# Mixture of softmaxes on one core: joint weights per unit, manual waits, larger edge loads, and the prior in the load queue

## Chip, cores, metric

One core of one Trainium2 chip. The metric is the device time of one execution in microseconds (us), read as the median of several; most executions of one kernel agree within 0.1 to 0.4 us here.

## The reference

```python
# logits [32, 128, 4, 4096] f32, prior [32, 128, 4] f32
prior_probs = softmax(prior, axis=-1)                  # over the 4 heads
softmax     = softmax(logits, axis=-1)                 # over the 4096 words
mixture     = np.sum(prior_probs[..., None] * softmax, axis=2)   # [32, 128, 4096]
```

268 MB are read and 67 MB written, each byte once.

## The kernel before

The 4096 rows are cut into 32 units of 128 rows, one row a partition. A unit is 4 heads x 4096 words = 8 MB of logits; its output is 2 MB. Two load buffers (`ltile`) alternate. ACT takes exp of a head and its sum (`dsum`), DVE the reciprocal, POOL multiplies it with the prior's weight (`coeff`), and DVE adds the weighted head to the output.

```python
def pieces(b):
    return 1 if b == 0 or b >= B - 3 else H        # heads per load: 2 MB pieces at the edges, else 8 MB
def load(b, eng=nc.sync):
    lt = lpool.tile([P, H, V], FP32, name="ltile")
    n = pieces(b)
    for h in range(0, H, n):
        eng.dma_start(out=lt[:, h : h + n], in_=lg[b // J, b % J, :, h : h + n, :])
...
load(0, eng=nc.sync)
nc.scalar.dma_start(out=pr, in_=pv)                # the prior, 64 KB, on ACT's queue
load(1, eng=nc.sync)
... # softmax of the prior on DVE and ACT, transposed to pp
ebuf = cpool.tile([P, 2, V], FP32, name="ebuf")
for b in range(B):
    ...
    if 0 < b < B - 3:
        store(b - 1, eng=nc.scalar)
    for h in range(H):
        et = lt[:, h] if inplace else ebuf[:, h % 2]
        ex = nc.scalar.activation(et, lt[:, h], AF.Exp, accum_out=dsum[:, col])
        ...
        nc.vector.reciprocal(rden[:, col], dsum[:, col])
        if h == 0:
            nc.vector.tensor_scalar(out=acc, in0=et, scalar1=rden[:, col], scalar2=pp[...],
                                    op0=ALU.mult, op1=ALU.mult)
            continue
        nc.gpsimd.tensor_mul(coeff[:, col], rden[:, col], pp[...])
        ... # scalar_tensor_tensor: acc = et * coeff + acc; the very last one in two halves, each stored
    if b + 2 < B:
        load(b + 2)
    if b == B - 3:
        store(b - 1); store(b)                     # from here on SP's queue
    elif b == B - 2:
        store(b)
```

The softmax here doesn't subtract the row's maximum and nothing guards it: scores larger than these inputs give would overflow.

## Time and profile before

| | before |
|---|---|
| time, median | 782.5 us (782.68 in the rounds with the changed kernel) |
| profiled span | 780.6 us |
| DVE, ACT, POOL busy | 68%, 60%, 2% |
| the two data queues, share of 16 DMA engines | 82.2% + 17.6% |
| DMA rate in the middle | 434 GB/s |
| first packet, last packet | 1.0 us, 779.2 us |

How to read it: a packet is one row's piece of a transfer, moved by one of the 16 DMA engines.

### The profile page before, as it was taken

The page shows a single profiled execution, that of the slowest core. Times are in us where ns is not written, and L with a number is a line of the kernel's source. Part 1 is how long each engine was busy: PE and PEld are TensorE (multiplying, and loading weights), DVE is VectorE, ACT ScalarE, POOL GpSimd, SP SyncE. Part 2 cuts the span into 40 slices and gives each one's busy share as a digit, 9 for nine tenths or more (in the row PEclk, how much of TensorE's full clock was granted, in tenths as well). Part 3 has the DMA queues.
Part 4 walks back from the last instruction along what each step waited for, and adds up shares of the span by engine and source line. Part 5 has one row for each costly group of instructions (what it writes and reads, how often), then busy time and mean ns, then how long its engine had stood idle before and what let it go on. Part 6 is the DMA issues. An engine that isn't in the chain of part 4 may idle for free.

```text
span 780.6 us, 853 instructions
## 1 busy us (share of the span) xinstructions
DVE 531.4 (68%) x266; ACT 470.2 (60%) x258; POOL 19.3 (2%) x101
## 2 busy tenths in 40 slices
DVE  5756668656686666866667765677666776668994
ACT  4376555755557655576555775457655567558971
POOL 0000000000000000000000000000000000000000
DMA  9999999999999999999999999999999999999998
GB/s 388 434 454 433 403 470 403 467 407 442 431 415 458 413 460 403 453 421 460 413 442 444 400 459 413 453 424 449 411 456 417 453 416 424 449 413 430 429 429 359
DMA packets 11127, 335.67 MB, mean 430 GB/s; under 512 B 1248, under 2 KB 1248, under 8 KB 1264
## 3 DMA queue, kind: packets, MB, share of 16 engines
q1 hardware_dynamic: 7056, 276.83, 82.2%
q10 hardware_dynamic: 4064, 58.79, 17.6%
q14 instruction: 7, 0.06, 0.0%
HBM read 268.50 MB, written 67.11 MB: 430 GB/s over the span
## 4 chain that ended last, share of the span: by engine, by line
DMA 66%; ACT 14%; DVE 10%; issue 7%; POOL 0%; SPq 0%; DVEq 0%; POOLq 0%; ACTq 0%
DMA ltile<-in_logits_dram 66%; ACT ebuf L135 14%; DVE acc L156 9%; DVE ltile L156 1%; POOL coeff L151 0%; SPq L75 0%; DVE rden L144 0%; DVEq L194 0%; DVE ltile L146 0%; POOLq L194 0%; ACTq L135 0%
## 5 line engine op out<-in xcount | busy, mean ns | idle before, releaser
L135 ACT ACTIVATE ebuf<-ltile 128x4096 f32<-128x4096 f32 x120 | 433.0, 3609 | 281.3 <-DMA ltile<-in_logits_dram 234.5
L156 DVE SCALAR_TENSOR_TENSOR acc<-ebuf,coeff,acc 128x4096 f32<-128x4096 f32 x90 | 403.6, 4484 | 27.3 <-POOL coeff L151 27.3
L144 DVE RECIPROCAL rden<-dsum 128x1 f32<-128x1 f32 x128 | 20.4, 160 | 200.7 <-ACT ebuf L135 200.7
L146 DVE TENSOR_SCALAR acc<-ebuf,rden,pp 128x4096 f32<-128x4096 f32 x30 | 72.4, 2412 | 1.1
L151 POOL TENSOR_TENSOR coeff<-rden,pp 128x1 f32<-128x1 f32 x96 | 18.2, 189 | 746.2 <-DVE rden L144 746.2
L135 ACT ACTIVATE ltile<-ltile 128x4096 f32<-128x4096 f32 x8 | 28.9, 3609 | 4.2 <-DMA ltile<-in_logits_dram 4.2
L156 DVE SCALAR_TENSOR_TENSOR ltile<-ltile,coeff 128x4096 f32<-128x4096 f32 (+1 forms) x7 | 27.0, 3874 | 1.8 <-POOL coeff L151 1.8
L135 ACT ACTIVATION_READ_ACCUMULATOR ebuf<-ltile 128x1 f32 x120 | 22.4, 186 | 0.0
L93 DVE TENSOR_REDUCE pmax<-pr 16x256 f32<-16x1024 f32 x1 | 1.2, 1207 | 7.0 <-DMA pr<-in_prior_dram 7.0
L95 ACT ACTIVATE pr<-pr 16x1024 f32<-16x1024 f32 x1 | 1.1, 1056 | 7.0 <-DVE pr L94 7.0
L146 DVE TENSOR_SCALAR ltile<-ltile,rden,pp 128x4096 f32<-128x4096 f32 x2 | 4.8, 2414 | 0.1
L98 DVE TENSOR_TENSOR pn<-pr,pmax 16x1024 f32<-16x1024 f32 x1 | 1.9, 1945 | 0.1
L95 ACT ACT_TABLE_LOAD x1 | 1.3, 1283 | 1.2 <-PEq L183 1.2
L96 DVE TENSOR_REDUCE pmax<-pr 16x256 f32<-16x1024 f32 x1 | 1.2, 1207 | 1.1 <-ACT pr L95 1.1
L105 DVE STREAM_TRANSPOSE pp<-pn 32x256 f32<-32x256 f32 x4 | 1.7, 435 | 0.1
L97 DVE RECIPROCAL pmax<-pmax 16x256 f32<-16x256 f32 x1 | 1.7, 1741 | 0.0
L135 ACT ACTIVATION_READ_ACCUMULATOR ltile<-ltile 128x1 f32 x8 | 1.5, 186 | 0.0
L94 DVE TENSOR_TENSOR pr<-pr,pmax 16x1024 f32<-16x1024 f32 x1 | 1.2, 1214 | 0.0
L91 POOL MEMSET pn<- 32x1024 f32 x1 | 0.9, 941 | 0.3 <-POOLq L183 0.3
L183 POOL MEMSET const-float32-0.0<- 128x1 f32 x1 | 0.1, 103 | 0.2 <-issue 0.2
L183 POOL MEMSET const-bfloat16-1.0<- 128x1 bf16 x1 | 0.1, 106 | 0.0
L183 POOL MEMSET const-uint8-127<- 128x1 uint8 x1 | 0.1, 106 | 0.0
(1 smaller groups left out, 0.1 us busy)
## 6 DMA issues: line engine op xcount, KB each, us to landing
out_dram<-acc ACTq DMA_DIRECT2D x28, 2048.0 KB, 29.3
ltile<-in_logits_dram SPq DMA_DIRECT2D x16, 2048.0 KB, 20.3
out_dram<-acc SPq DMA_DIRECT2D x2, 2048.0 KB, 32.9
out_dram<-ltile SPq DMA_DIRECT2D x1, 2048.0 KB, 21.2
out_dram<-ltile SPq DMA_DIRECT2D x2, 1024.0 KB, 8.7
ltile<-in_logits_dram SPq DMA_DIRECT2D x28, 32.3
pr<-in_prior_dram ACTq DMA_DIRECT2D x1, 64.0 KB, 6.2
```

The costliest lines, as they stand in the source:

```text
L93: nc.vector.reduce_max(pmax, pr, axis=AX.X)
L94: nc.vector.tensor_sub(pr, pr, pmax.unsqueeze(2).to_broadcast([G, R, H]))
L95: nc.scalar.activation(pr, pr, AF.Exp)
L96: nc.vector.reduce_sum(pmax, pr, axis=AX.X)
L97: nc.vector.reciprocal(pmax, pmax)
L98: nc.vector.tensor_mul(pn[0:G].rearrange("g h r -> g r h"), pr, pmax.unsqueeze(2).to_broadcast([G, R, H]))
L105: nc.vector.transpose(pp[32 * t : 32 * (t + 1)], pq[:, :, :, 32 * t : 32 * (t + 1)])
L135: ex = nc.scalar.activation(et, lt[:, h], AF.Exp, accum_out=dsum[:, col])
L144: nc.vector.reciprocal(rden[:, col], dsum[:, col])
L146: nc.vector.tensor_scalar(out=acc, in0=et, scalar1=rden[:, col], scalar2=pp[:, b % J, h, b // J : b // J + 1], op0=ALU.mult, op1=ALU.mult,)
L151: nc.gpsimd.tensor_mul(coeff[:, col], rden[:, col], pp[:, b % J, h, b // J : b // J + 1])
L156: nc.vector.scalar_tensor_tensor(out=acc[:, cs], in0=et[:, cs], scalar=coeff[:, col], in1=acc[:, cs], op0=ALU.mult, op1=ALU.add,)
```

## The change

Its intent: one reciprocal and one coefficient per unit (per two heads in the last four units), waits declared by hand so that each instruction waits for one or two things only, the first head's exp in place and the other three in three buffers of their own (one in PSUM), pieces of two heads for the edge units, and the prior's load on SP's queue between the two halves of unit 0. The first weighted add of a unit now also frees its load buffer.

```diff
+    nc.at_finalize(early_first_load)
-        return 1 if b == 0 or b >= B - 3 else H
+        if u == 0 or u >= U - 3:
+            cuts = (0, 2, 3, 4) if u == U - 1 else (0, 2, 4)
+        else:
+            cuts = (0, H)
+            if u >= 2:
+                only(ld, adds[u - 2, 0] if h == 0 else exps[u - 2, to - 1])
+            if u == 0 and h == 0:
+                nc.sync.dma_start(out=pr, in_=pv)
-    nc.scalar.dma_start(out=pr, in_=pv)
-    ebuf = cpool.tile([P, 2, V], FP32, name="ebuf")
+    ebuf1 = cpool.tile([P, V], FP32, name="ebuf1")
+    ebuf2 = psum.tile([P, V], FP32, name="ebuf2")
+    ebuf3 = cpool.tile([P, V], FP32, name="ebuf3")
+    obuf = cpool.tile([P, 2, V], FP32, name="obuf")
...
+            def weigh(h, n, *keep):
+                rc = nc.vector.reciprocal(rden[:, u, h : h + n], dsum[:, u, h : h + n])
+                only(rc, exps[u, h + n - 1])
+                mul = nc.gpsimd.tensor_mul(
+                    coeff[:, u, h : h + n], rden[:, u, h : h + n], ppu[:, h : h + n])
+                return only(mul, rc, *keep)
...
+            free = (stores[u - 2],) if bufd and u >= 2 else ()
+            m = H if u < U - 4 else 2
+            for h in range(H):
+                if h == H - 1 and 0 < u < U - 3:
+                    store(u - 1, obuf[:, (u - 1) % 2], nc.scalar)
+                exp(h, *((stores[u - 4],) if late else ()))
+                if (h + 1) % m:
+                    continue
+                g = h + 1 - m
+                mul = weigh(g, m, *(free if g == 0 else ()))
+                ... # the weighted adds of heads g to h
```

`only(ins, *keep)` keeps the waits named and drops the others.

More of the change, by code (lines that the diff above doesn't have):

```diff
@@ L53 @@
     G = B * S // R
-    B = G * J
-    assert G * R == B * S and G <= 32
+    U = G * J
+    assert G * R == B * S and G <= 32 and H == 4
     lg = logits.rearrange("b s h v -> (b s) h v").rearrange("(g p j) h v -> g j p h v", p=P, j=J)
@@ L59 @@
     pv = prior.rearrange("b s h -> (b s) h").rearrange("(g r) h -> g r h", r=R)
-    lpool = ctx.enter_context(tc.tile_pool(name="lpool", bufs=2))
-    apool = ctx.enter_context(tc.tile_pool(name="apool", bufs=2))
     cpool = ctx.enter_context(tc.tile_pool(name="cpool", bufs=1))
-    def pieces(b):
-        return 1 if b == 0 or b >= B - 3 else H
-    ltiles = {}
-    def load(b, eng=nc.sync):
-        lt = lpool.tile([P, H, V], FP32, name="ltile")
-        n = pieces(b)
-        for h in range(0, H, n):
-            eng.dma_start(out=lt[:, h : h + n], in_=lg[b // J, b % J, :, h : h + n, :])
-        ltiles[b] = lt
@@ L78, with only @@
-    accs = {}
-    def store(b, lo=0, hi=V, eng=nc.sync):
-        eng.dma_start(out=ov[b // J, b % J, :, lo:hi], in_=accs[b][:, lo:hi])
-    load(0, eng=nc.sync)
-    nc.at_finalize(early_first_load)
+    psum = ctx.enter_context(tc.tile_pool(name="psum", bufs=1, space=bass.MemoryType.PSUM))
+    before = {}
+    def only(ins, *keep):
+        for k in keep:
+            tc.add_manual_dep(
+                ins.ins,
+                k.ins.name,
+                mybir.DependencyInfo(mybir.DependencyClass.Sync, mybir.DependencyReason.DATA),
+                reason="all that this instruction waits for",
+            )
+        tc.declare_no_dep(
+            ins.ins,
+            group="loop",
+            keep=[k.ins for k in keep] + before.get(ins.ins.engine, []),
+            reason="covered by the waits that are kept",
+        )
+        tc.add_to_no_dep_group("loop", ins.ins)
+        before[ins.ins.engine] = [ins.ins]
+        return ins
@@ new lines, with load @@
+    ltile = cpool.tile([P, 2, H, V], FP32, name="ltile")
+    loads = {}
+    exps = {}
+    adds = {}
+    stores = {}
+    def load(u):
+        if u == 0 or u >= U - 3:
+            cuts = (0, 2, 3, 4) if u == U - 1 else (0, 2, 4)
+        else:
+            cuts = (0, H)
+        for h, to in zip(cuts, cuts[1:]):
+            ld = nc.sync.dma_start(
+                out=ltile[:, u % 2, h:to], in_=lg[u // J, u % J, :, h:to, :]
+            )
+            if u >= 2:
+                only(ld, adds[u - 2, 0] if h == 0 else exps[u - 2, to - 1])
+            else:
+                only(ld)
+            for k in range(h, to):
+                loads[u, k] = ld
+            if u == 0 and h == 0:
+                nc.sync.dma_start(out=pr, in_=pv)
@@ L87, with store @@
+    def store(u, acc, eng, lo=0, hi=V):
+        st = eng.dma_start(out=ov[u // J, u % J, :, lo:hi], in_=acc[:, lo:hi])
+        stores[u] = only(st, adds[u, H - 1])
     pr = cpool.tile([G, R, H], FP32, name="pr")
-    nc.scalar.dma_start(out=pr, in_=pv)
-    load(1, eng=nc.sync)
     pn = cpool.tile([32, H, R], FP32, name="pn")
-    nc.gpsimd.memset(pn, 0.0)
     pmax = cpool.tile([G, R], FP32, name="pmax")
-    nc.vector.reduce_max(pmax, pr, axis=AX.X)
-    nc.vector.tensor_sub(pr, pr, pmax.unsqueeze(2).to_broadcast([G, R, H]))
@@ L95 @@
-    nc.scalar.activation(pr, pr, AF.Exp)
-    nc.vector.reduce_sum(pmax, pr, axis=AX.X)
-    nc.vector.reciprocal(pmax, pmax)
-    nc.vector.tensor_mul(
-        pn[0:G].rearrange("g h r -> g r h"), pr, pmax.unsqueeze(2).to_broadcast([G, R, H])
-    )
-    pq = pn.rearrange("g h (p j) -> g j h p", j=J)
-    pp = cpool.tile([P, J, H, 32], FP32, name="pp")
-    for t in range(P // 32):
-        nc.vector.transpose(pp[32 * t : 32 * (t + 1)], pq[:, :, :, 32 * t : 32 * (t + 1)])
-    NCHUNK = 2
-    dsum = cpool.tile([P, B * H], FP32, name="dsum")
@@ L111 @@
-    rden = cpool.tile([P, B * H], FP32, name="rden")
-    coeff = cpool.tile([P, B * H], FP32, name="coeff")
-    ebuf = cpool.tile([P, 2, V], FP32, name="ebuf")
-    exps = []
-    for b in range(B):
-        last = b == B - 1
-        inplace = b >= B - 2
-        lt = ltiles.pop(b)
-        if not inplace:
-            accs[b] = apool.tile([P, V], FP32, name="acc")
-        else:
-            accs[b] = lt[:, 0]
-        acc = accs[b]
-        if 0 < b < B - 3:
-            store(b - 1, eng=nc.scalar)
-        for h in range(H):
-            split = last and h == H - 1
-            i = b * H + h
-            col = slice(i, i + 1)
-            et = lt[:, h] if inplace else ebuf[:, h % 2]
-            ex = nc.scalar.activation(et, lt[:, h], AF.Exp, accum_out=dsum[:, col])
-            if h == 0:
-                tc.keep_in_program_order(ex)
-            if not inplace:
-                if len(exps) >= 2:
-                    tc.declare_no_dep(ex.ins, exps[-2], reason="covered by the sum")
-                exps.append(ex.ins)
-            nc.vector.reciprocal(rden[:, col], dsum[:, col])
-            if h == 0:
-                nc.vector.tensor_scalar(
-                    out=acc, in0=et, scalar1=rden[:, col], scalar2=pp[:, b % J, h, b // J : b // J + 1],
-                    op0=ALU.mult, op1=ALU.mult,
-                )
-                continue
-            nc.gpsimd.tensor_mul(coeff[:, col], rden[:, col], pp[:, b % J, h, b // J : b // J + 1])
-            n = NCHUNK if split else 1
-            w = V // n
-            for c in range(n):
-                cs = slice(c * w, (c + 1) * w)
-                nc.vector.scalar_tensor_tensor(
-                    out=acc[:, cs], in0=et[:, cs], scalar=coeff[:, col], in1=acc[:, cs],
-                    op0=ALU.mult, op1=ALU.add,
-                )
-                if split:
-                    store(b, c * w, (c + 1) * w)
-        if b + 2 < B:
-            load(b + 2)
-        if b == B - 3:
-            store(b - 1)
-            store(b)
-        elif b == B - 2:
-            store(b)
@@ new lines, with exp, add @@
+    pp = cpool.tile([P, J, H, 32], FP32, name="pp")
+    dsum = cpool.tile([P, U, H], FP32, name="dsum")
+    rden = cpool.tile([P, U, H], FP32, name="rden")
+    coeff = cpool.tile([P, U, H], FP32, name="coeff")
+    ebuf1 = cpool.tile([P, V], FP32, name="ebuf1")
+    ebuf2 = psum.tile([P, V], FP32, name="ebuf2")
+    ebuf3 = cpool.tile([P, V], FP32, name="ebuf3")
+    obuf = cpool.tile([P, 2, V], FP32, name="obuf")
+    with tc.manual_schedule():
+        load(0)
+        load(1)
+        nc.gpsimd.memset(pn, 0.0)
+        nc.vector.reduce_max(pmax, pr, axis=AX.X)
+        nc.vector.tensor_sub(pr, pr, pmax.unsqueeze(2).to_broadcast([G, R, H]))
+        nc.scalar.activation(pr, pr, AF.Exp)
+        nc.vector.reduce_sum(pmax, pr, axis=AX.X)
+        nc.vector.reciprocal(pmax, pmax)
+        nc.vector.tensor_mul(
+            pn[0:G].rearrange("g h r -> g r h"), pr, pmax.unsqueeze(2).to_broadcast([G, R, H])
+        )
+        pq = pn.rearrange("g h (p j) -> g j h p", j=J)
+        for t in range(P // 32):
+            nc.vector.transpose(pp[32 * t : 32 * (t + 1)], pq[:, :, :, 32 * t : 32 * (t + 1)])
+        for u in range(U):
+            bufd = u < U - 2
+            lt = ltile[:, u % 2]
+            acc = obuf[:, u % 2] if bufd else lt[:, 0]
+            es = (lt[:, 0], ebuf1, ebuf2, ebuf3) if bufd else [lt[:, h] for h in range(H)]
+            ppu = pp[:, u % J, :, u // J]
+            def exp(h, *keep):
+                ex = nc.scalar.activation(
+                    es[h], lt[:, h], AF.Exp, accum_out=dsum[:, u, h : h + 1]
+                )
+                keep = (loads[u, h],) + keep
+                if bufd and h and u:
+                    keep += (adds[u - 1, h],)
+                exps[u, h] = only(ex, *keep)
+            def weigh(h, n, *keep):
+                rc = nc.vector.reciprocal(rden[:, u, h : h + n], dsum[:, u, h : h + n])
+                only(rc, exps[u, h + n - 1])
+                mul = nc.gpsimd.tensor_mul(
+                    coeff[:, u, h : h + n], rden[:, u, h : h + n], ppu[:, h : h + n]
+                )
+                return only(mul, rc, *keep)
+            def add(h, mul, lo=0, hi=V):
+                if h == 0:
+                    st = nc.vector.tensor_scalar(
+                        out=acc[:, lo:hi], in0=es[h][:, lo:hi], scalar1=coeff[:, u, h : h + 1],
+                        scalar2=None, op0=ALU.mult,
+                    )
+                    adds[u, h] = only(st, mul)
+                else:
+                    st = nc.vector.scalar_tensor_tensor(
+                        out=acc[:, lo:hi], in0=es[h][:, lo:hi], scalar=coeff[:, u, h : h + 1],
+                        in1=acc[:, lo:hi], op0=ALU.mult, op1=ALU.add,
+                    )
+                    adds[u, h] = only(st, mul, adds[u, h - 1])
+            free = (stores[u - 2],) if bufd and u >= 2 else ()
+            m = H if u < U - 4 else 2
+            for h in range(H):
+                late = h == H - 1 and 4 <= u < U - 3
+                if h == H - 1 and 0 < u < U - 3:
[5 more added lines that the diff above has]
+                mul = weigh(g, m, *(free if g == 0 else ()))
+                for k in range(g, h + 1):
+                    n = 2 if u == U - 1 and k == H - 1 else 1
+                    w = V // n
+                    for c in range(n):
+                        add(k, mul, c * w, (c + 1) * w)
+                        if n > 1:
+                            store(u, acc, nc.sync, c * w, (c + 1) * w)
+            if u + 2 < U:
+                load(u + 2)
+            if u == U - 3:
+                store(u - 1, obuf[:, (u - 1) % 2], nc.sync)
+                store(u, acc, nc.sync)
+            elif u == U - 2:
+                store(u, acc, nc.sync)
```

## The prediction

> **What bounds the kernel now.** I read the page's busy shares first, then the DMA queues, then stretches of the span, then the waits of the issuing queue, and last the order of work at the end.
>
> ```profile
> DVE 531.4 (68%) x266; ACT 470.2 (60%) x258; POOL 19.3 (2%) x101
> DMA  9999999999999999999999999999999999999998
> ...
> q1 hardware_dynamic: 7056, 276.83, 82.2%
> q10 hardware_dynamic: 4064, 58.79, 17.6%
> q14 instruction: 7, 0.06, 0.0%
> HBM read 268.50 MB, written 67.11 MB: 430 GB/s over the span
> ```
>
> No compute engine is near full, while the two data queues together take 82.2 + 17.6 = 99.8% of the time of 16 DMA engines. Every byte is needed (logits in once, output out once), and the change leaves all of them. So the next question is only where the DMA engines are not at their best rate. By stretch (columns: stretch, length, busy time of DVE, ACT and POOL, clock, DMA share, GB/s):
>
> ```profile
> 0.00:3.00 3.00, 0.00 (x0) 1.28 (x1) 1.15 (x5) 1.00 0.70 208
> 3.00:12.00 9.00, 3.84 (x4) 2.54 (x2) 0.00 (x0) 1.00 1.00 408
> 100.40:680.90 580.50, 390.84 (x193) 349.46 (x193) 13.64 (x72) 1.00 1.00 434
> 681.00:753.00 72.00, 60.41 (x29) 55.37 (x31) 2.08 (x11) 1.00 1.00 430
> 753.00:771.00 18.00, 16.81 (x10) 8.61 (x6) 0.57 (x3) 1.00 1.00 428
> 771.00:777.00 6.00, 0.00 (x0) 0.00 (x0) 0.00 (x0) 1.00 1.00 425
> 777.00:779.50 2.50, 0.00 (x0) 0.00 (x0) 0.00 (x0) 1.00 0.21 88
> ```
>
> The middle holds 434 GB/s without a hole. What isn't that: about 1 us before the first packet, a slow start of about another us, 72 us at 430 where the last units load in 2 MB pieces, and an end where the share falls to 0.21. The packet records in the trace give the reason for the last two. A 16 KB packet (a row of a 2 MB piece or of a store) takes 611 ns, a 64 KB packet (a row of an 8 MB load) 2418 ns: four small ones cost 2444. The first DMA engines finish at 777.2 us and one alone goes on to 779.2; its lag grows in steps after each of the seven instruction packets of q14 (309 ns each, at 147, 165, 349, 471, 486, 736 and 750 us), and 7 x 309 = 2.2 us. So the end is that of one DMA engine that also fetches instructions.
>
> The waits of the queue that issues loads, and the issues at the end:
>
> ```profile
> SPq L75 <- ACT ebuf L135: 464.1, 30, 16.0
> ...
> 663.66 0.33 SPq L75 DMA_DIRECT2D ltile<-in_logits_dram  x1
> ...
> 669.65 0.34 ACTq L81 DMA_DIRECT2D out_dram<-acc  x1
> 671.78 3.62 ACT L135 ACTIVATE ebuf<-ltile 128x4096 f32<-128x4096 f32 x1 [8.14 <-DMA ltile<-in_logits_dram]
> ...
> 753.55 17.57 SPq L81 DMA_DIRECT2D out_dram<-ltile  x3
> ```
>
> A load is asked for 8 us before the one ahead of it lands (663.66 against 671.78), so loads queue up. The "chain that ended last" gives 14% to ACT and 10% to DVE, but this is how it walks back; DMA was busy throughout, and those shares are not time to be won.
>
> **What the Trainium skill says.** "DMA: Bandwidth & Descriptors", section "Where 436 GB/s comes from", puts the ceiling of 16 engines at 435.2 GB/s; this trace has 434 in the middle, so it agrees and no headroom is left there. The same page, "Issuing engines are not separate DMA queues", says DMAs from different engines share the same 16 DMA engines and interleave; the 99.8% above agrees, so moving the prior from ACT's queue to SP's wins no bandwidth. Its "Queues, rings and completion order" says each engine alternates between queues packet by packet: a 2 MB store is 8 packets an engine, each beside one load packet, 8 x (0.611 + 2.418) = 24.2 us, and the page shows 29.3 us from issue to landing. "Runtime: NRT & Kernel Launch", "Instruction fetch mechanics", says the sequencer fetches its next page over its own DMA queue and that this is mostly hidden; here it is hidden from the engines but not from the one DMA engine that carries it.
>
> **The change, part by part.**
> 1. Joint weights. For units 0 to 27 one reciprocal and one coefficient replace four and three; for the last four, two and two replace four and three. Reciprocals go from 128 to 28 + 8 = 36 (160 ns each, 14.7 us less DVE), coefficients from 96 to 36 (189 ns, 11.3 us less POOL, and 60 waits of 0.3 us less on DVE). All lies beside DMA: 0 us directly. But it is 152 instructions less, with 7 load issues and some wait instructions on top, of 853. In proportion, 13 instruction packets (7 in the span, 6 before it) lose some 2 of those in the span: 0.6 us off the lagging engine. Estimate 0.3 to 0.9.
> 2. Larger pieces: unit 0, 29 and 30 in two, unit 31 in three. Per unit an engine moves 8 x 2444 = 19.55 us in 16 KB packets and 8 x 2418 = 19.34 in 64 KB ones; 32 KB should lie at 19.42. Gain 3 x 0.13 + 0.07, about 0.4 us.
> 3. The first weighted add now waits for all four exps and the load after next waits for that add. From landing: 4 x 3.6 (exp) + 0.35 (store issue on ACT before the last exp) + 0.6 (reciprocal, coefficient) + 2.41 = 17.8 us, against 16.1 (687.84 - 671.78) now; the next landing is at 24.2. Slack 6.4 us in place of 8.1.
> 4. The store is issued before the last exp of the next unit, at 10.9 us after its landing, instead of 2.1 us before it: 13 us later. It lands at 24.2 + 10.9 + 29.3 = 64.4 us after its unit's landing. The coefficient of the unit two later waits for it: 48.3 + 15.1 = 63.4. So that comes 1 us late, the load's slack falls to about 5 us. Take off about 3 for issue latency and write receipt and it is still positive. If it were not, the store then in flight still has about half of its 4.9 us of packets to fill the hole. Middle: 0 us.
> 5. Prior behind 4 MB: it arrives at about 12.8 us instead of 6.97, so the first exp begins at about 16.4 instead of 10.42, and the third load is asked for at about 34 instead of 28.5. Two loads are 38.7 us of DMA work, dry at about 41. Start: 0 us.
> 6. End. SP's queue is in order: unit 31's loads, stores 28, 29, 30, then two halves of 31. The pieces of 31 land at about 749.5 (both heads), 754.5, 759.4. Exps of 3.62 each, one after another: 749.7 to 764.2. Joint coefficient at 764.9. Adds: 4.48 to 769.4, then halves of 2.3 to 771.7 and 774.0. Now they end at 768.5 and 770.8, so the last store half is issued 3.3 us later. Does it show? Engines without fetches are through with everything before it at 771.9; they idle for about 1 us, move half a (2.5 us) from 772.9 to 775.4, then b to 777.9. The lagging engine has its backlog until 773.5, moves a to 776, b to 778.5. Thus the end is at about 778.3 instead of 779.2; the 2 us of lag hide the later adds.
>
> Sum: -0.6 (fetches) - 0.4 (pieces) + 0.3 (idle at the end that the lag only partly hides) = -0.7 us, from 782.5 to 781.8.
>
> **Rivals.**
> - *A load comes late and DMA idles in the middle.* For it: parts 3 and 4 put two more waits ahead of each load, and 29.3 is a median. Against it: 5 us of slack, and a store always in flight. Were 1 us lost in each of 28 units, time would be 810.
> - *The tail is longer than the lag hides.* For it: only some 1 us separates the two in part 6, and instruction fetches that vanish make the lag smaller. Each us of later adds beyond it costs 1 us: up to 784.
> - *ebuf in PSUM slows the adds.* The trace has no such instruction. Even 2 us more on one add of a unit leaves DVE at 18.5 of 24.2 us, and the last two units don't use it: 0 us.
> - *Removing 92 reciprocals and 60 coefficients pays directly.* The chain with 24% on engines speaks for it; the DMA share of 1.00 in each stretch speaks against. It would make 760 or less, under what 335.67 MB take at 434 GB/s (773.4 us): impossible.
>
> **Range and chances.** The gain is bounded: all DMA work is kept, so at best the 2 us of lag and 1 us of piece overhead go: 780. A tail 2 us worse makes 784. Both lie far inside 2% (15.7 us). Only the first rival could leave it. Prediction 781.8, range 780.4 to 783.6; faster by 2% 0.01, within 0.97, slower 0.02.
>
> **What would show it.** Right: DMA share 1.00 and 433 to 434 GB/s from 100 to 680 us; about five instruction packets; q1 with 976 packets fewer (896 rows and 7 x 16 completions of loads gone, 32 of the prior come in); waits of DVE on POOL much rarer; the first exp at about 16 us; the last store half issued at about 774; the last packet before 779. Wrong: a slice with a digit below 9 between the third and the last, or loads in the middle landing more than 24.2 us apart.

## The result, and the profile after

781.07 us (780.98 to 781.43, 6 runs) against 782.68 (782.52 to 782.79, 6 runs). A ratio is the mean time of one kernel's runs over that of the other's of the same rounds, so not quite the ratio of the medians quoted: 0.998, 95% interval 0.9967 to 0.9993. That is within 2%, and inside the range of the prediction; the gain of 1.6 us is twice the 0.7 forecast.

The page of the changed kernel, its busy times and its DMA queues:

```profile
DVE 521.0 (67%) x174; ACT 466.5 (60%) x258; POOL 8.4 (1%) x41
DMA  9999999999999999999999999999999999999998
...
q1 hardware_dynamic: 6080, 276.89, 82.3%
q10 hardware_dynamic: 4032, 58.72, 17.6%
q14 instruction: 5, 0.04, 0.0%
```

DVE has 92 instructions less and POOL 60, and the span shrinks by 1.3 us only: 780.6 to 779.3. q1 has 976 packets less, as counted ahead, and there are five instruction packets for seven. By stretch (length, busy time of DVE, ACT and POOL, clock, DMA share, GB/s):

```profile
100.40:680.90 580.50, 383.64 (x120) 347.51 (x193) 4.87 (x24) 1.00 1.00 433
681.00:753.00 72.00, 60.88 (x23) 50.18 (x29) 1.39 (x7) 1.00 0.99 426
771.00:777.00 6.00, 2.43 (x2) 0.00 (x0) 0.00 (x0) 1.00 0.98 408
777.00:779.50 2.50, 0.00 (x0) 0.00 (x0) 0.00 (x0) 1.00 0.07 26
```

The middle is what it was, 433 for 434. Packets are counted where they start, so single stretches scatter by a few GB/s. The last stretch has a share of 0.07 where the kernel before had 0.21: there the time was won. The order of work in the middle, and the waits between 100 and 681 us (us in total, times, longest):

```profile
662.51 0.33 SPq L100 DMA_DIRECT2D ltile<-in_logits_dram  x1
...
669.26 3.62 ACT L160 ACTIVATE ltile<-ltile 128x4096 f32<-128x4096 f32 x1 [9.66 <-DMA ltile<-in_logits_dram]
...
676.08 0.34 ACTq L115 DMA_DIRECT2D out_dram<-obuf  x1
...
680.07 3.60 ACT L160 ACTIVATE ebuf<-ltile 128x4096 f32<-128x4096 f32 x1
```

```profile
POOL coeff L171 <- DVE rden L169: 575.7, 24, 24.4
ACT ltile L160 <- DMA ltile<-in_logits_dram: 233.0, 24, 10.1
```

The load is asked for 6.75 us before the next landing (669.26 - 662.51), where the prediction had 6.4 and the kernel before has 8.1. The store goes out 6.8 us after the landing, not 10.9: in the program it stands before the last exp (680.07), but ACT's sequencer issues it while the exps ahead of it still wait in the engine. So it lands in time, and in the middle no coefficient waits for a store: all 24 waits of POOL are for DVE.

The end before, then after (each from its own timeline):

```profile
766.15 4.61 DVE L156 SCALAR_TENSOR_TENSOR ltile<-ltile,coeff 128x2048 f32<-128x2048 f32 x2 [0.30 <-POOL coeff L151]
768.52 2.60 SPq L81 DMA_DIRECT2D out_dram<-ltile  x2
```

```profile
764.30 9.13 DVE L184 SCALAR_TENSOR_TENSOR ltile<-ltile,coeff 128x4096 f32<-128x4096 f32 x3 [0.31 <-POOL coeff L171]
771.20 2.60 SPq L115 DMA_DIRECT2D out_dram<-ltile  x2
```

The last two stores are issued 2.7 us later than before, and yet the kernel ends 1.3 us earlier. The completion records of the 16 DMA engines tell why. This table is worked out from the trace's packet records (us, the first and the last of the 16 engines; the lag is the last less the first; instruction packets are those of 8 KB in the span), for these two kernels and for experiments told below:

```
kernel                   instr.   store of unit 30 done   last store done    lag at
                         packets  first     last          first    last      unit 30
before                    7       772.2     774.3         777.2    779.2     2.1
after                     5       771.8     773.1         777.0    778.0     1.3
heads apart again         6       771.9     773.8         777.7    778.7     1.9
512 memsets on POOL       9       771.8     774.9         778.2    779.8     3.1
1024 memsets on POOL     13       771.7     777.0         780.5    781.9     5.3
before, larger pieces     6       771.7     773.9         776.7    778.9     2.2
512 memsets, POOL + DVE   9       771.9     774.6         779.1    779.8     2.7
weights apart at the end  5       771.8     772.9         776.7    777.8     1.1
```

The first engines are through with unit 30 0.4 us earlier (larger pieces), then idle some 0.3 us for the later adds; the last engine lags 1.3 us instead of 2.1.

Which engine carries which instruction packet (a fetch) can be worked out too. In these records a packet begins 3 or 4 ns before the one ahead of it on its engine ends, and an engine moves 8 of the 128 rows of each transfer. Strung together so, the records of twelve traces (all but the two with later loads) fall into 16 whole chains, one an engine (in the first 20 us packets overlap, and the stringing is looser). A fetch costs its engine its own 309 ns and what the packet behind it takes beyond the usual (of the experiments, the chains that matter):

```
kernel                  fetches in one chain, us (cost of each)         chain's last packet
before                  146.7, 486.1 (0.84, 0.85)                       779.2
                        164.8, 470.6, 749.7 (0.55, 0.56, 0.69)          779.1
                        735.9 (0.72)                                    778.8
                        349.2 (0.53)                                    777.8
after                   147.9, 511.2 (0.55, 0.56)                       778.0
                        193.9 (0.84)                                    777.9
                        774.9 (0.45)                                    777.8
                        704.7 (0.40)                                    777.5
heads apart again       125.5, 513.3 (0.84, 0.84)                       778.7
512 memsets on POOL     105.5, 275.3, 445.2, 615.0, 753.6 (0.53-0.66)   779.8
512 memsets, POOL + DVE 102.4, 342.1, 579.3 (0.84, 0.90, 0.84)          779.5
                        153.8, 468.7, 734.1 (0.53, 0.56, 0.58)          779.2
```

So before, not one engine ends late but three, at 778.8 to 779.2, and the next one at 777.8. Each chain carries the fetches of one instruction stream, by this count: 512 memsets bring four packets, so a packet holds 128 instructions. With heads apart DVE has 8 instructions a unit, 128 in 16 units or 387 us, and 513.3 - 125.5 is 388. The chain whose fetches cost 0.84 us or more is DVE's by this count; in the kernel before I take it for DVE's because of the same cost. Its fetches fall from two to one with the change, and an engine with two cheaper fetches is last instead. Why a fetch costs more on DVE's engine is open.

### The profile page after: what moved, and what is told of

Read it like the earlier page. It is cut to its first block, busy times and chain, and to the rows that moved or that the text cites. A ratio compares the mean times of both kernels' runs of the same rounds, so it can differ in the third digit from the quotient of the medians.

```text
span 779.3 us, 655 instructions
## 1 busy us (share of the span) xinstructions
DVE 521.0 (67%) x174; ACT 466.5 (60%) x258; POOL 8.4 (1%) x41
## 4 chain that ended last, share of the span: by engine, by line
DMA 63%; ACT 28%; DVE 6%; issue 2%; POOL 0%; DVEq 0%; POOLq 0%
DMA ltile<-in_logits_dram 59%; ACT ebuf L160 19%; ACT ltile L160 8%; DVE obuf L178 5%; DMA out_dram<-obuf 2%; DMA pr<-in_prior_dram 2%; DVE ltile L184 1%; POOL coeff L171 0%; DVE rden L169 0%; DVEq L241 0%; DVE pr L141 0%; DVE pmax L140 0%; ACT pr L142 0%; POOLq L241 0%; POOLq L171 0%
## 5 line engine op out<-in xcount | busy, mean ns | idle before, releaser
L184 DVE SCALAR_TENSOR_TENSOR obuf<-ebuf,coeff,obuf 128x4096 f32<-128x4096 f32 x90 | 403.6, 4484 | 3.8 <-POOL coeff L171 0.6
L160 ACT ACTIVATE ebuf<-ltile 128x4096 f32<-128x4096 f32 x90 | 322.9, 3588 | 5.0 <-DMA ltile<-in_logits_dram 5.0
L160 ACT ACTIVATE ltile<-ltile 128x4096 f32<-128x4096 f32 x38 | 137.3, 3614 | 278.0 <-DMA ltile<-in_logits_dram 278.0
L169 DVE RECIPROCAL rden<-dsum 128x4 f32<-128x4 f32 (+1 forms) x36 | 6.3, 175 | 221.9 <-ACT ebuf L160 219.1
L178 DVE TENSOR_SCALAR obuf<-ltile,coeff 128x4096 f32<-128x4096 f32 x30 | 70.6, 2353 | 11.0 <-POOL coeff L171 11.0
L160 ACT ACTIVATION_READ_ACCUMULATOR ebuf<-ltile 128x1 f32 x90 | 16.8, 186 | 0.0
L171 POOL TENSOR_TENSOR coeff<-rden,pp 128x4 f32<-128x4 f32 (+1 forms) x36 | 7.3, 202 | 755.3 <-DVE rden L169 744.6
L160 ACT ACTIVATION_READ_ACCUMULATOR ltile<-ltile 128x1 f32 x38 | 7.1, 186 | 0.0
L178 DVE TENSOR_SCALAR ltile<-ltile,coeff 128x4096 f32<-128x4096 f32 x2 | 4.7, 2353 | 0.6 <-POOL coeff L171 0.6
## 6 DMA issues: line engine op xcount, KB each, us to landing
out_dram<-obuf ACTq DMA_DIRECT2D x28, 2048.0 KB, 29.4
```

What stands on the lines that cost most here:

```text
L160: ex = nc.scalar.activation(es[h], lt[:, h], AF.Exp, accum_out=dsum[:, u, h : h + 1])
L169: rc = nc.vector.reciprocal(rden[:, u, h : h + n], dsum[:, u, h : h + n])
L171: mul = nc.gpsimd.tensor_mul(coeff[:, u, h : h + n], rden[:, u, h : h + n], ppu[:, h : h + n])
L178: st = nc.vector.tensor_scalar(out=acc[:, lo:hi], in0=es[h][:, lo:hi], scalar1=coeff[:, u, h : h + 1], scalar2=None, op0=ALU.mult,)
L184: st = nc.vector.scalar_tensor_tensor(out=acc[:, lo:hi], in0=es[h][:, lo:hi], scalar=coeff[:, u, h : h + 1], in1=acc[:, lo:hi], op0=ALU.mu ...
```

## The experiments

Theory, as held then: DMA work sets the time, ended by the one DMA engine that lags because of instruction fetches. Rivals: the instructions and waits themselves; the prior's place; the adds at the end. All kernels gave correct results. The kernel before ran in the same rounds of each, at 782.59 to 782.67 us; its 95% intervals of ratios are about 0.12% (1 us) to either side, so I lean on the runs themselves, which for one kernel mostly scatter by 0.2 to 0.5 us.

**1. Heads apart again in units 0 to 27.** With single weights the first add no longer comes after all exps, so a load has to wait for the last exp as well.

```diff
-            m = H if u < U - 4 else 2
+            m = 1 if u < U - 4 else 2
-                only(ld, adds[u - 2, 0] if h == 0 else exps[u - 2, to - 1])
+                keep = [adds[u - 2, 0] if h == 0 else exps[u - 2, to - 1]]
+                if h == 0:
+                    keep.append(exps[u - 2, to - 1])
+                only(ld, *keep)
```

> The changed kernel with one reciprocal and one coefficient per head again in units 0 to 27, the rest left alone. Theory (DMA work, and one DMA engine that also fetches instructions, set the time): the 168 instructions that come back are worth 1 to 2 more 8 KB instruction packets (6 or 7 in place of 5), so 0.3 to 0.6 us: 781.4 to 781.7. Rival (the instructions and waits themselves were on the path): DVE gets 84 x 160 ns and 84 waits of 0.3 us back, so the whole gain is lost or more: 782.7 and up.

Measured 781.64 us (781.53 to 782.01), 0.6 us over the changed kernel, with

```profile
q14 instruction: 7, 0.05, 0.0%
```

One of these seven is a 32-byte packet at 0.1 us; six are of 8 KB, one more than in the changed kernel. So it is one fetch more and 0.6 us, within what was expected of one or two. POOL's busy time goes from 8.4 to 24.1 us and DVE's from 521.0 to 526.9 and that is not what is paid; the lag is (1.9 us in the table): DVE's engine carries two fetches again and is last.

**2. Idle memsets on POOL, 512 and 1024.** Nothing waits for them.

```diff
+            for _ in range(16):                      # 32 in the second kernel
+                nc.gpsimd.memset(scratch, 0.0)
             if u + 2 < U:
                 load(u + 2)
```

> The changed kernel with 16 tiny memsets of a scratch column on POOL after each unit's weights, 512 in all, that nothing waits for. Theory: 512 instructions of 64 bytes are four 8 KB packets more (9 in place of 5); if they all run on the DMA engine that lags, its end moves by 4 x 0.31 = 1.2 us: 782.3. Rival (compute engines and their waits set the time): POOL is 1% busy and nothing waits: 781.1.

> As the run with 512 idle memsets, with 1024. Theory: eight packets more than the changed kernel (13), end later by 8 x 0.31 = 2.5 us: 783.5, twice the step of the run with 512. Rival: 781.1 still.

Measured 782.90 (782.70 to 783.07) and 785.22 (785.04 to 785.39): 1.8 and 4.1 us over the changed kernel, for

```profile
q14 instruction: 9, 0.07, 0.0%
```

```profile
q14 instruction: 13, 0.11, 0.0%
```

The packet counts are exact, and instructions that nothing waits for do cost time. The rival falls. But each packet costs some 0.5 us, not 0.31. The stretches of the kernel with 1024 show one reason:

```profile
100.40:680.90 580.50, 383.56 (x120) 344.75 (x191) 129.09 (x792) 1.00 1.00 433
...
771.00:777.00 6.00, 5.85 (x3) 0.00 (x0) 1.03 (x11) 1.00 0.45 188
777.00:779.50 2.50, 0.00 (x0) 0.00 (x0) 0.00 (x0) 1.00 1.02 419
```

The middle is untouched. Near the end the other DMA engines idle (share 0.45): a load counts as landed only when the last engine is done (in the changed kernel the first piece of unit 31 is complete on the first engine at 747.5 us, on the last at 748.8, and its exp begins at 749.2), so the lag delays the last exps and adds (DVE is busy 5.85 of 6 us there), and with them the last stores of all 16 engines. The other reason is in the packet records: across one POOL fetch the lag steps by 0.5 to 0.7 us (1.23 to 1.76, 1.76 to 2.38, 2.38 to 3.08 in the kernel with 512), more than the fetch's own 309 ns, as the load packet behind it takes 2634 to 2722 ns instead of 2418. And the lags of the engines grow apart: not every fetch adds to the largest one. So, against the prediction, the fetches do not all fall on one DMA engine.

**3. Small pieces again** (2 MB for units 0, 29, 30, 31).

```diff
-            cuts = (0, 2, 3, 4) if u == U - 1 else (0, 2, 4)
+            cuts = (0, 1, 2, 3, 4)
```

> The changed kernel with the small pieces of the kernel before (2 MB) for units 0, 29, 30 and 31. Theory: per unit of two 4 MB pieces an engine spends 8 x (4 x 611 - 2 x 1213) = 0.14 us more, in sum 0.5 us: 781.5. Rival (the chain of exps and adds of the last unit sets the end): the first head of the last unit lands some 5 us earlier, so the last add ends about 1 us earlier: 780.1.

Measured 782.09 us, in two groups: 781.42 and 781.45, and three from 782.09 to 782.32. The direction is the theory's, the rival's gain of 1 us isn't there, the size is 0.4 or 1.1 us where 0.5 was expected. The profiled run is of the faster group (span 779.6); what sets the slower one apart stays open.

**4. Later loads.** A whole-unit load waits for the second or the fourth add.

```diff
-                only(ld, adds[u - 2, 0] if h == 0 else exps[u - 2, to - 1])
+                only(ld, adds[u - 2, 1 if to == H else 0] if h == 0 else exps[u - 2, to - 1])   # or 3
```

> The changed kernel, but a whole-unit load waits for the second weighted add of the unit it overwrites, not the first: asked for some 4.5 us later (about 22 us after that unit's landing, 2 us before the next landing). Theory (DMA sets the time; there is slack, and a store in flight fills a short hole): within 0.5 us of the changed kernel, 781.1 to 781.6. Rival (the moment of the load's issue is on the path): 27 units x 4.5 us, 880 and up.

> The changed kernel, but a whole-unit load waits for the fourth weighted add: about 31 us after the unit's landing, past the next landing at 24 us. Here theory and rival agree that the DMA engines run dry: two units then take the time of a load and its compute, so some 4 to 8 us more a unit, 880 to 1000. It shows where the slack ends, and what a dry queue looks like in the profile.

Measured 794.66 us (793.53 to 795.71) and 914.98 (914.50 to 915.65). The second is as foreseen. Its stretch from 300 to 400 us:

```profile
300.00:400.00 100.00, 54.11 (x17) 50.08 (x27) 0.61 (x3) 1.00 0.86 354
```

The first is a miss for both: 13.6 us slower, where theory had under 0.5 and the rival 100. Its page and a stretch of its middle:

```profile
out_dram<-obuf ACTq DMA_DIRECT2D x28, 2048.0 KB, 22.6
```

```profile
300.00:500.00 200.00, 127.88 (x40) 119.20 (x66) 1.62 (x8) 1.00 1.00 427
```

The DMA share is still 1.00: the load queue runs dry for up to 1.0 us in most units, the store fills in and lands in 22.6 us instead of 29.4, and nobody idles. But in the packet records 817 of the 3584 load packets of 64 KB, all after 100 us, took over 2450 ns (3 after 100 us in the changed kernel), and the mean of all rose from 2420 to 2476 ns. 8 packets x 56 ns = 0.45 us a unit and DMA engine, x 28 units = 12.5 us, close to the 13.6 measured. So a load asked for too late costs time even where another queue fills the hole, and the busy share doesn't show it; the rate does. What makes the packets slow is not shown. Only 63 of the 817 begin within 4 us of their load's first packet; 616 begin within 8 us of the first packet of a store. The store queue, drained sooner, had mostly been empty for 5 to 10 us by then, against about 4 in the changed kernel.

**5. The prior on ACT's queue again.**

```diff
-                nc.sync.dma_start(out=pr, in_=pv)
+                nc.scalar.dma_start(out=pr, in_=pv)
```

> The changed kernel with the prior's load issued from ACT's queue again, as in the kernel before. Theory: the prior arrives 6 us earlier and the first exps begin earlier, but the load queue has work until 41 us anyway: 781.1, no change (within 0.2). Rival (the place of the prior in the load queue gave the gain): back towards 782.5.

Measured 780.99 us (780.87 to 781.01). No change, perhaps 0.1 us less. The prior's place gave nothing.

**6. Weights apart in the last unit.**

```diff
-            m = H if u < U - 4 else 2
+            m = H if u < U - 4 else 1 if u == U - 1 else 2
```

> The changed kernel with one weight per head in the last unit alone, so that its adds follow its exps sooner: the last add ends some 4 us earlier. Theory: the lagging DMA engine has its queue full to the end anyway, so 0 to 0.3 us are won: 780.8 to 781.1. Rival (the chain of exps and adds after the last load sets the end): 4 us won, 777.

Measured 781.48 us (781.45 to 781.88), 0.4 slower. The experiment didn't do what I had in mind: the adds did not come earlier, but 0.4 us later.

```profile
769.25 4.62 DVE L184 SCALAR_TENSOR_TENSOR ltile<-ltile,coeff 128x2048 f32<-128x2048 f32 x2 [0.30 <-POOL coeff L171]
771.63 2.60 SPq L115 DMA_DIRECT2D out_dram<-ltile  x2
```

I had overlooked that DVE was busy with unit 30 until 756 us and then had no hole left; two more reciprocal-and-coefficient steps only lengthen it. Nor can the 0.4 us be put down to the adds. Three of the five executions have a profiled span of 779.3 us, that of the changed kernel (the others 779.6 and 779.7); what is longer is the time outside the span, 2.1 to 2.2 us instead of 1.7 to 1.8. The kernel before has 2.1 us there as well, and why is open. So this run decides nothing about the adds.

**7. Weights apart in the last two units**, which gives DVE work before unit 30's last exp:

```diff
-            m = H if u < U - 4 else 2
+            m = H if u < U - 4 else 1 if u >= U - 2 else 2
```

> The changed kernel with one weight per head in the last two units, so that DVE starts the adds of unit 30 before its last exp and the last add ends 2 to 3 us earlier (771 in place of 773.4). Theory: the first 15 DMA engines then never wait for the last stores, but the one that lags had none to wait for: 0 to 0.3 us won, 780.8 to 781.1. Rival (the adds after the last load set the end): 2 us won or more, 779.

Measured 780.98 us (780.92 to 781.15). The last store half is issued about 1.9 us earlier, and 0.1 us is won at most: not told apart from the changed kernel, and the rival's 2 us are not there. Earlier adds don't help: in both kernels the engine that ends last has no gap in its packets to the end, so it waits for no add.

**8. That, and two-head weights in unit 1**, so that the load of unit 3 comes before its queue runs dry:

```diff
+            m = 2 if u == 1 else H if u < U - 4 else 1 if u >= U - 2 else 2
```

> The run before, and two-head weights in unit 1 as well, so that the load of unit 3 is asked for some 3 us earlier and its queue doesn't run dry at 60 us (its first packets took 2650 to 2820 ns there, not 2418). Theory: 0.2 to 0.3 us a DMA engine beyond the run before: 780.5 to 780.9. Rival (a queue that runs dry costs nothing while a store fills in): no change against the run before.

Measured 781.12 us (781.07 to 781.20). The load was issued at 56.3 us instead of 59.2, and the slow packets near 60 us fell from 0.33 to 0.07 us an engine, but 0.29 us of slow packets appeared near 48 us, where the first store begins. The sum is unchanged and so is the time. Whether an isolated dry moment can be avoided at all stays open.

**9. The kernel before with the larger pieces alone.**

```diff
-        n = pieces(b)
-        for h in range(0, H, n):
-            eng.dma_start(out=lt[:, h : h + n], in_=lg[b // J, b % J, :, h : h + n, :])
+        cuts = (0, H) if pieces(b) == H else (0, 2, 3, 4) if b == B - 1 else (0, 2, 4)
+        for h, to in zip(cuts, cuts[1:]):
+            eng.dma_start(out=lt[:, h:to], in_=lg[b // J, b % J, :, h:to, :])
```

> The kernel before with one part of the change: units 0, 29 and 30 loaded in two pieces and unit 31 in three. Theory: an engine has some 0.5 us less of packets, the lag of the last DMA engine stays at 2 us: 0.4 to 0.5 us under the kernel before, 782.2. Rival (pieces don't matter, joint weights alone gave the gain): no change, 782.65.

Measured 782.00 us (781.90 to 782.15) against 782.59 (782.46 to 782.81): 0.6 us, and the runs of the two don't overlap (the ratio, 0.9992, has an interval of 0.9979 to 1.0005 that holds 1). In the table the first engines gain 0.5 us, the last packet 0.3, and the lag stays at 2.2. The span shrinks by 0.3 us as well (780.5 to 780.2); the other 0.3 lie outside it, where this kernel has 1.8 us and the kernel before 2.1. So this part works alone, but only 0.3 us of it are seen in the trace.

**10. 512 memsets, half on POOL, half on DVE.**

```diff
+            for _ in range(8):
+                nc.gpsimd.memset(scratch, 0.0)
+                nc.vector.memset(scratch2, 0.0)
```

> The changed kernel with 512 idle memsets as before, but half on POOL and half on DVE (8 and 8 after each unit's weights). Revised theory (each instruction stream is fetched over a DMA engine of its own, about 0.6 us of lag a fetch, and the engine with the largest lag sets the end): four packets more, as with 512 on POOL, but two on each engine: 781.9 to 782.3. Rival (the theory as first stated: one DMA engine carries all fetches, only their number counts): as with 512 on POOL, 782.9.

Measured 783.13 us (782.94 to 783.17), which by the number would be the rival's. But the 8 memsets of unit 30 and 31 stand in DVE's way at the end:

```profile
766.35 9.13 DVE L186 SCALAR_TENSOR_TENSOR ltile<-ltile,coeff 128x4096 f32<-128x4096 f32 x3 [0.31 <-POOL scratch L212]
773.25 2.60 SPq L115 DMA_DIRECT2D out_dram<-ltile  x2
```

The last adds end 2 us later than in the changed kernel, the first DMA engines idle for them and end at 779.1 us instead of 777.0. The forecast of the time failed for that, and the time decides nothing. The chains decide for the revised theory: the nine fetches lie in four chains, and two of them have grown from one fetch to three (DVE's, and another that must be POOL's), so two more on each and not four on one. The largest lags at unit 30 are 2.7, 1.7 and 1.2 us, where 512 on POOL alone gave 3.1, 1.25 and 1.0.

## Why the prediction was right

- **Bound and direction.** Right. DMA share 1.00 in the middle before and after, and 152 fewer reciprocals and coefficients give nothing directly: memsets that nothing waits for move the time and the prior's place doesn't.
- **Part 1, fetches (-0.6).** The mechanism is right, the mechanics are wrong, and that the size fits is partly luck. Two packets less was exact. But "one alone goes on to 779.2" and "its lag grows in steps after each of the seven instruction packets" misread the trace: three engines end late, the last carries two of the seven fetches, and these cost 0.84 us each, not 0.31. What the change took from that engine is one such fetch; then the next engine, 0.9 us over the middle one in place of 1.8, is the last. Of the 1.2 us that the last packet comes earlier, single weights put back 0.6 and the larger pieces alone give 0.3; the rest I did not isolate. Hand-declared waits may have a share (before has 42 waiting instructions of DVE's sequencer, after has 4), which is not shown.
- **Part 2, larger pieces (-0.4).** Right: 0.4 us for the first engines between the two kernels; done alone on the kernel before 0.6 us of time, of which 0.3 lie in the profiled span.
- **Part 3, slack of the load.** Right in size (6.75 us against 6.4). The fallback argued in part 4, that the store in flight would fill a hole, failed: asking for the load 4.5 us later costs 13.6 us, in slower packets and not in idle time. The prediction was right here because the slack held, not because of the fallback.
- **Part 4, the store.** Wrong: it is issued 6.8 us after the landing, not 10.9, as its place in the program doesn't hold back the sequencer. So the 1 us that the coefficient was to come late doesn't exist. It didn't matter.
- **Part 5, prior.** Right: the first exp begins at 16.45 us (about 16.4 forecast), and the time is 781.0 to 781.1 with the prior on either queue.
- **Rival, ebuf in PSUM.** Refuted: the 90 adds that read the three buffers take 4484 ns in the mean, as the 90 of the kernel before do.
- **Part 6, the end (+0.3).** Right in kind: the last engine's backlog hid the later adds. The first engines idled for 0.3 us, not 1; the adds ended at 773.4, not 774.0. Adds 1.9 us earlier win 0.1 us at most. What adds a little later would cost is not shown.
- **Sum.** -0.7 forecast, -1.6 measured. Of this the trace shows 1.3 (the first engines 0.2, the lag 1.0, rounding the rest); 0.3 us lie outside the profiled span and are not explained; the larger pieces alone bring the same 0.3.

No version beat the changed kernel clearly: the prior on ACT's queue and the weights apart in the last two units are both 0.1 us under it, inside the scatter.

## What to carry to other kernels

When the DMA share is 1.00 all through, count packets and look at which of the 16 DMA engines ends last, as a load or a store has landed only when the slowest has. Removing instructions then pays through their fetches alone, here 0.4 to 0.9 us each, and only if the stream they are removed from is the one whose engine ends last. Ask for loads early enough even if another queue keeps the engines busy: the busy share stays at 1.00 while the rate falls. A change at the end of a kernel is worth only what the longer of two ends leaves, so find both (here the adds and the lagging DMA engine) before shortening one. And compare the profiled spans too: here 0.3 to 0.4 us of a difference in time lay outside them.

## What the Trainium skill lacked or had wrong

- "Runtime: NRT & Kernel Launch", "Instruction fetch mechanics", calls fetching mostly hidden. In a kernel at 433 GB/s it isn't: eight more 8 KB instruction packets cost 4.1 us, and one of 309 ns sets the DMA engine that carries it back by 0.4 to 0.9 us. The page doesn't say that one stream's fetches all fall on one DMA engine, as they do in the twelve traces strung into chains. The page has blocks of 16 KiB; packets here are of 8 KB, four for 512 instructions.
- No page has the cost of a load that is asked for too late while another queue fills in: 64 KB load packets went from 2420 to 2476 ns in the mean, 13.6 us in all, at a DMA share of 1.00.
- "Advanced Engine Details and Errata", "Sequencer and Instruction Queues", says that a sequencer pushes engine instructions into a queue and reads on; the runs agree, but the consequence for DMA issues isn't drawn: a store placed before the fourth exp went out 4.0 us before that exp began (676.08 and 680.07).
